# Forgetting attention in pairs of heads: rows 0 to 63 and 64 to 127 of the array, and norm-spreading products over all 128 rows

## The chip, the cores and the metric

The kernel runs on one core of a Trainium2 chip, in one launch. The metric is the device time of that launch in microseconds, and the median of three runs is compared. TensorE (PE in the profile) multiplies, VectorE is DVE, ScalarE is ACT, GpSimd is POOL, and SyncE (SP) issues the loads of the weights. PSUM, where products land, has eight banks.

## The reference

Ten sublayers work on 256 tokens of 1024 channels: feed-forward, forgetting attention ("fox"), two feed-forwards, dilated attention ("dil"), a feed-forward, and then twice a mixing layer and a second kind of feed-forward. The change is about the attention. For each of 16 heads of 64 channels, forgetting attention computes

```python
q, k = rms_norm(q) * q_gain, rms_norm(k) * k_gain      # each head by itself, 64 channels
F = cumsum(log_sigmoid(x @ w_f + b_f))                 # one running sum per head
logits = q @ k.T / 8 + F[queries, None] - F[None, keys]
out = softmax(where(key <= query, logits, -inf)) @ v
```

Dilated attention has the same norm of each head's queries and keys, with three sets of them, and no running sums.

## The kernel before

Activations stand with channels on the 128 partitions and tokens along the free axis. A weight tile is split into a part that float32r holds (`whi`) and the rest (`wlo`), and so are the activations (`hh`, `hl`), so that each float32 product is three float32r ones of 128x256. Each such triple stands in the trace as `banks<-hh,whi`, `hl,whi` and `hh,wlo` (or `whi,hh`, and `oh`, `ol` for attention's outputs). 1024 KB of weights come at a time from SP's queue, four loads ahead; ACT makes `whi` and DVE `wlo`, up to seven units ahead of PE. These projections are the main stream of PE.

What is not a projection runs beside them, as generators. After every few projections `step` asks each generator whether it can emit its next instructions; it asks a planner (`Clock`), which keeps an estimate of each engine's time from shapes alone. So the program order on each engine follows from that estimate, and a change of one generator moves others too. Every instruction is issued by one helper, so that all lines of the trace are L415 (L416 in the changed kernel, where comments went).

In `fox`, a pair of heads shares one tile of queries and keys: head 2c on partitions 0 to 63, head 2c + 1 on 64 to 127. `head_in` squares it and transposes the squares (`cst,hsq`) for the mean squares. `head_norm` works out 1 / rms for two pairs at once (three in `dil`), transposes it (`cst,ypad`), and spreads it over the channels by products with 0/1 matrices: for each pair two products `banks<-yz,sel` of 128x256, of which eight rows of the array are used (rows 32i to 32i + 7 for pair i). There are 8 such pairs in `fox` and 24 in `dil`, 64 products in all.

`fox_head` then does one head: for two tiles of queries, q times k over 64 rows (`banks<-qk`, 64x128 and 64x256; a float32 product is two instructions on PE) and a bfloat16 product over 6 rows that adds the running sums (`banks<-ar` 6x128 and 6x256, tiles E and F, which `fox_sums` fills by small DMAs on POOL's queue); DVE adds the mask and takes the row's maximum; ACT takes the exponential with its sum; three transposes (`cst,ar` 128x128), which ACT copies to `pT`; values times `pT` into 64 partitions of PSUM (`pv`: `ar` 128*64, four instructions); and the inverse sums brought to the same shape (`inverse`: `cst,rs`, four instructions). `turn` lets one head at a time through the part from the transposes on, since there is one `pT`. `o_store` scales the outputs of a pair (`ot`), splits them into `oh` and `ol`, and `attn_out` multiplies them with four chunks of weights; chunk c waits for the pairs 2c and 2c + 1.

Of the kernel before, what the change touches and what calls it, by code (L numbers as in the profile page):

```python
# [66 lines left out]
def _weights(seg):  # L67
    """Chunks of one part of the network, each of one or two units: (key, number of units)."""
# [58 lines left out]

# which layer's modulation is worked out beside which of the first blocks
# [102 lines left out]
# columns of the tile that holds one value per channel  # L231
# [9 lines left out]
# columns of the tile of constants  # L241
_CST = {}
_n = 0
for _name, _w in (("ident", 128), ("ones", 1), ("two", 2), ("part", 1), ("perm", 128), ("causal", 384), ("nc", 256), ("ns", 256), ("cmask", 32), ("valid", 2), ("invf", 1),
# [5 lines left out]
# columns of the small matrices of a mixing layer  # L250
# [8 lines left out]
def _ch(v):  # L259
    """[..., n * 128] -> [128, prod(...) * n]"""  # L260
# [30 lines left out]
def _host_cst():  # L291
# [16 lines left out]
    row = np.arange(128) % 32  # L308
    sel = [(row[:, None] < 8) & (row[:, None] % 4 == w * 2 + np.arange(128)[None, :] // 64) for w in range(2)]
# [5 lines left out]
    c["nc"] = np.cos(ang)[:, d % 32].T  # L315
    c["ns"] = np.sin(ang)[:, d % 32].T * np.where(d < 32, -1.0, 1.0)[:, None]
# [15 lines left out]
    return np.ascontiguousarray(np.concatenate([c[n].reshape(128, w) for n, (_, w) in _CST.items()], axis=1), np.float32), dm, sel  # L332
# [62 lines left out]
class Engine:  # L395
    """An engine's instructions, with an estimate of when they are done."""
# [24 lines left out]
class Clock:  # L421
    """Passes instructions on to the core's engines, and estimates (in ns) when their operands are there and
# [1846 lines left out]
```

## Time and profile before

| | us |
|---|---|
| median of 3 runs (1941.72 to 1943.92) | 1943.55 |
| profiled execution, span | 1946.9 |
| PE busy (97%) | 1891.6 |
| DVE busy (76%) | 1488.4 |
| ACT busy (52%) | 1013.4 |
| forgetting attention, from the norm's scale to the last sum | about 222 to 379 |
| dilated attention, the same | about 771 to 1115 |

The profile is of one execution, whose span is 3.35 us above the median of the runs. A matmul's duration in it is modelled and includes the time through the array, so that busy time says little of how fast matmuls follow each other. The distance from one start to the next does.

### The profile page before, as it was taken

How to read it: one execution, taken by the hardware profiler on the slowest of the kernel's cores; microseconds unless marked ns; L12 is line 12 of the kernel's file. 1: busy time of each engine (PE TensorE's matmuls, PEld its weight loads, DVE VectorE, ACT ScalarE, POOL GpSimd, SP SyncE). 2: the span in 40 equal slices, each digit the busy share in tenths (PEclk: the TensorE clock that was granted, in tenths of full speed). 3: DMA queues.
4: the chain of work that ended last, by engine and by line, in shares of the span. 5: the costliest groups of instructions: out<-in, count | busy, mean ns of one | idle time of the engine just before them, and what ended most of it. 6: DMA issues, size and time to landing. Idle time of an engine off the chain costs nothing.

```text
span 1946.9 us, 36564 instructions
## 1 busy us (share of the span) xinstructions
PE 1891.6 (97%) x15150; PEld 1814.4 (93%) x15150; DVE 1488.4 (76%) x2706; ACT 1013.4 (52%) x1721; POOL 35.5 (2%) x40
## 2 busy tenths in 40 slices
PE   6999999999999999999999999999999998999997
PEld 6999987899999999999989899999889998989997
DVE  6987795598779876767777585569779778969876
ACT  3534644554355445554455464444666555466553
POOL 0100000000000000000000000000000000000000
PEclk9999989999999999999999999999989998999998
DMA  9798373289858973433324175535236543325550
GB/s 373 298 350 322 131 282 109 93 306 362 326 178 298 341 298 130 174 115 125 130 88 143 74 261 205 212 130 188 94 128 217 186 157 127 137 84 191 199 195 23
DMA packets 54167, 378.67 MB, mean 194 GB/s; under 512 B 6096, under 2 KB 7600, under 8 KB 9072
## 3 DMA queue, kind: packets, MB, share of 16 engines
q1 hardware_dynamic: 52992, 373.20, 52.2%
q0 software_dynamic: 864, 3.00, 0.5%
q8 instruction: 118, 1.93, 0.4%
q14 instruction: 49, 0.40, 0.1%
q10 hardware_dynamic: 144, 0.13, 0.0%
HBM read 375.21 MB, written 1.05 MB: 193 GB/s over the span
## 4 chain that ended last, share of the span: by engine, by line
PE 72%; issue 20%; DVE 4%; ACT 2%; POOL 1%; DMA 0%; POOLq 0%; SPq 0%; DVEq 0%; ACTq 0%
PE banks L415 72%; DVE ar L415 1%; DVE wlo L415 1%; POOL rz L415 1%; DVE x L415 1%; ACT whi L415 1%; ACT hh L415 0%; DVE sq L415 0%; DMA x<-x 0%; DVE hl L415 0%; DVE ht L415 0%; ACT sq L415 0%; ACT L415 0%; DVE wraw L415 0%; ACT ar L415 0%
## 5 line engine op out<-in xcount | busy, mean ns | idle before, releaser
L415 PE MATMUL banks<-hh,whi 128*128 128x256 f32 (+1 forms) x2792 | 799.2, 286 | 7.6 <-ACT hh L415 4.7
L415 DVE TENSOR_TENSOR wlo<-wraw,whi 128x1024 fp32r<-128x1024 f32 x557 | 670.2, 1220 | 171.2 <-ACT whi L415 170.6
L415 PE MATMUL banks<-hh,wlo 128*128 128x256 f32 (+1 forms) x2792 | 789.4, 283 | 2.0 <-DVE wlo L415 2.0
L415 PE MATMUL banks<-hl,whi 128*128 128x256 f32 (+1 forms) x2792 | 790.1, 283 | 0.2
L415 ACT CAST whi<-wraw 128x1024 fp32r<-128x1024 f32 x557 | 570.3, 1048 | 177.5 <-DMA wraw<-w 92.2
L415 PEld LDWEIGHTS banks<-hh,whi 128*128 128x128 f32 x2792 | 531.2, 190 | 13.5 <-ACT hh L415 5.5
L415 PEld LDWEIGHTS banks<-hh,wlo 128*128 128x128 f32 x2792 | 531.2, 190 | 2.8 <-DVE wlo L415 2.8
L415 PEld LDWEIGHTS banks<-hl,whi 128*128 128x128 f32 x2792 | 531.4, 190 | 1.1 <-DVE hl L415 1.1
L415 PE MATMUL banks<-oh,whi 128*128 128x256 f32 x1312 | 372.7, 284 | 7.3 <-DVE x L415 3.8
L415 PE MATMUL banks<-ol,whi 128*128 128x256 f32 x1312 | 366.8, 280 | 0.0
L415 PE MATMUL banks<-oh,wlo 128*128 128x256 f32 x1312 | 366.4, 279 | 0.0
L415 PEld LDWEIGHTS banks<-oh,whi 128*128 128x128 f32 x1312 | 247.2, 188 | 14.0 <-DVE x L415 6.3
L415 PEld LDWEIGHTS banks<-ol,whi 128*128 128x128 f32 x1312 | 247.5, 189 | 0.2 <-DVE ol L415 0.2
L415 PEld LDWEIGHTS banks<-oh,wlo 128*128 128x128 f32 x1312 | 247.2, 188 | 0.0
L415 DVE CUSTOM_DVE_ANT_0 wraw<-wraw,cb 128x1024 f32<-128x1024 f32 x128 | 152.0, 1217 | 0.5 <-DMA wraw<-w 0.5
L415 ACT ACTIVATE sg<-banks 128x256 f32<-128x256 f32 x82 | 31.5, 385 | 175.4 <-PE banks L415 175.3
L415 PE MATMUL banks<-whi,hh 128*128 128x256 f32 x352 | 106.0, 301 | 1.6 <-ACT hh L415 1.4
L415 PE MATMUL banks<-whi,hl 128*128 128x256 f32 x352 | 101.3, 288 | 0.1
L415 PE MATMUL banks<-wlo,hh 128*128 128x256 f32 x352 | 100.9, 287 | 0.0
L415 ACT COPY ar<-banks 128x384 f32<-128x384 f32 (+5 forms) x110 | 47.4, 477 | 99.3 <-PE banks L415 96.0
L415 PE MATMUL banks<-ar 128*64 128x256 f32 (+4 forms) x456 | 90.9, 335 | 0.0
L415 DVE SCALAR_TENSOR_TENSOR cy<-cs,vec,cy 128x255 f32<-128x255 f32 (+1 forms) x176 | 83.7, 481 | 7.8 <-ACT cy L415 4.7
(204 smaller groups left out, 1790.5 us busy)
## 6 DMA issues: line engine op xcount, KB each, us to landing
wraw<-w SPq DMA_DIRECT2D x342, 1024.0 KB, 4.9
ar<-w SPq DMA_DIRECT2D x8, 1024.0 KB, 10.4
wraw<-w SPq DMA_DIRECT2D x5, 512.0 KB, 3.4
ar<-lw POOLq DMA_DIRECT2D x2, 752.0 KB, 5.0
x<-x SPq DMA_DIRECT2D x1, 1024.0 KB, 7.2
out<-x SPq DMA_DIRECT2D x8, 128.0 KB, 1.9
cst<-cst SPq DMA_DIRECT2D x1, 595.5 KB, 6.1
ar<-dm POOLq DMA_DIRECT2D x1, 576.0 KB, 10.4
```

The source lines that it names most:

```text
L415: return f(out, *args, **kw)
```

## The change

- `fox_heads` takes the place of `fox_head` and does two heads: the products of head 2c (rows 0 to 63) and of head 2c + 1 (rows 64 to 127) alternate, into two neighbouring banks of PSUM. E and F have the running sums of a pair on partitions 0 to 5 and 64 to 69, zeros elsewhere in each half, so these products take 64 rows.
- `pv2` and `inverse2` alternate between the two heads too, which fill partitions 0 to 63 and 64 to 127 of one bank.
- The transposes come before the wait for `turn`, and there are two `pT`s, each for a pair.
- The products that spread the norms take all 128 rows: `sel` holds, for each pair, zeros but for that pair's rows (768 columns, not 256), and the unused rows of `ypad` are transposed along.
- The DMAs of E and F are 12 of 4 KB, not 6 of 8 KB, and the fills of E and F six, not two. The tables of the rotation leave the constants (256 KB less there) and are loaded into `cb` when the first mixing layer begins; `sel` is loaded and copied with 256 KB more. Comments went.

```diff
-    sel = [(row[:, None] < 8) & (row[:, None] % 4 == w * 2 + ...) for w in range(2)]
+    sel = [(row // 32 == i) & (row % 32 < 8) & (row % 4 == w * 2 + ...)
+           for i in range(3) for w in range(2)]
...
     def head_norm(self, qks, v):
-        m = 32 * n
         for tt in range(2):
-            nc.tensor.transpose(yT[:m, tt * 128:tt * 128 + 128],
-                                yp[:, tt * n:tt * n + n].rearrange("p x c -> p (x c)"), self.c("ident"))
+            nc.tensor.transpose(yT[:, tt * 128:tt * 128 + 128],
+                                self.ypad[:, tt * n:tt * n + 4].rearrange("p x c -> p (x c)"), self.c("ident"))
...
-                nc.tensor.matmul(rb[:, w * S:w * S + S], self.sel[32 * i:32 * i + 8, w * 128:w * 128 + 128],
-                                 z[32 * i:32 * i + 8], start=True, stop=True)
+                nc.tensor.matmul(rb[:, w * S:w * S + S], self.sel[:, (2 * i + w) * 128:(2 * i + w) * 128 + 128],
+                                 z, start=True, stop=True)
...
+    def inverse2(self, out, rs):
+        for qt in range(2):
+            for e in range(2):
+                self.nc.tensor.matmul(out[64 * e:64 * e + 64, qt * 128:qt * 128 + 128],
+                                      rs[:, 2 * e + qt:2 * e + qt + 1].to_broadcast([128, 64]), self.c("ident"), ...)
...
-    def fox_head(self, h, qk, fv, vready, E, F, pvs):
+    def fox_heads(self, c, qk, fv, vready, E, F, pvs):
-        L = yield from self.bank()
+        L = yield from self.bank(2)
         for qt, c0, n in blocks:
             q = slice(qt * 128, qt * 128 + 128)
-            nc.tensor.matmul(L[:, c0:c0 + n], qk[r, q], qk[r, S:S + n], start=True, stop=False)
-            nc.tensor.matmul(L[:, c0:c0 + n], E[:, h, q], F[:, h, :n], start=False, stop=True)
+            for e, r in enumerate(half):
+                nc.tensor.matmul(L[:, e, c0:c0 + n], qk[r, q], qk[r, S:S + n], start=True, stop=False)
+            for e, r in enumerate(half):
+                nc.tensor.matmul(L[:, e, c0:c0 + n], E[r, c, q], F[r, c, :n], start=False, stop=True)
...
-        while self.turn != h:
+        for e in range(2):
+            yield from self.on("pe", P[:, e])
+            ... three transposes, ACT's copy into pT[:, e]
+        while self.turn != c or not vready[c // 2]:
             yield
...
+    def pv2(self, out, parts):
+        for i, (v, pT, kt) in enumerate(parts):
+            for e in range(2):
+                o = out[64 * e:64 * e + 64]
+                q, p = (o[:, 128:S], pT[:, e, 256:384]) if kt else (o[:, :S], pT[:, e, :256])
+                self.nc.tensor.matmul(q, v[e], p, start=i == 0, stop=i == len(parts) - 1, ...)
...
-            nc.gpsimd.dma_start(E[3 + i:4 + i], part[:, :S])
-            nc.gpsimd.dma_start(F[i:i + 1], part[:, S:])
+            for e in range(2):
+                o = 64 * e + i
+                nc.gpsimd.dma_start(E[o + 3:o + 4], part[e:16:2, :S])
+                nc.gpsimd.dma_start(F[o:o + 1], part[e:16:2, S:])
...
+        if l == 0:
+            nc.gpsimd.dma_start(self.cb[:, :2 * S], self.a["turn"])
...
-                k.nc.gpsimd.dma_start(k.ar[:, 0:256], k.a["sel"])
-                k.nc.scalar.copy(k.sel, k.ar[:, 0:256])
+                k.nc.gpsimd.dma_start(k.ar[:, 0:768], k.a["sel"])
+                k.nc.scalar.copy(k.sel, k.ar[:, 0:768])
```

PE, where a head's output products (`ar`), its inverse sums (`rs`), the next head's transposes (`cst,ar`) and logits (`qk`, and `ar` for E and F) follow each other, before:

```order
L415 MATMUL banks<-ar 64x256
L415 MATMUL banks<-ar 64x128
L415 MATMUL banks<-cst,rs 64x128 x2
L415 MATMUL banks<-cst,ar 128x128 x3
L415 MATMUL banks<-qk 128x128
L415 LDWEIGHTS ar
L415 MATMUL banks<-ar 128x128
L415 MATMUL banks<-qk 128x256
L415 LDWEIGHTS ar
L415 MATMUL banks<-ar 128x256
```

PE at the same work now, the output products of one pair (the last of them) and the logits of a later pair:

```order
L416 MATMUL banks<-ar 64x128 x2
L416 MATMUL banks<-cst,rs 64x128 x4
L416 MATMUL banks<-qk 128x128 x2
L416 LDWEIGHTS ar
L416 MATMUL banks<-ar 128x128
L416 LDWEIGHTS ar
L416 MATMUL banks<-ar 128x128
L416 MATMUL banks<-qk 128x256 x2
L416 LDWEIGHTS ar
L416 MATMUL banks<-ar 128x256
L416 LDWEIGHTS ar
L416 MATMUL banks<-ar 128x256
```

The two heads of a pair alternate row by row, and the transposes have moved away from between outputs and logits. Twice in the middle of the stage the outputs of two pairs and the logits of the next two pairs stand in one run like this.

ACT, the exponentials (`ar,sums<-ar,nm`) of the fifth and the sixth pair and the copies of their transposes, now:

```order
L416 ACTIVATE ar,sums<-ar,nm 128x128
L416 ACTIVATE ar,sums<-ar,nm 128x256
L416 ACTIVATE ar,sums<-ar,nm 128x128
L416 ACTIVATE ar,sums<-ar,nm 128x256
L416 COPY ar<-banks 128x384
L416 ACTIVATE ar,sums<-ar,nm 128x128
L416 ACTIVATE ar,sums<-ar,nm 128x256
L416 ACTIVATE ar,sums<-ar,nm 128x128
L416 ACTIVATE ar,sums<-ar,nm 128x256
L416 COPY ar<-banks 128x384
```

Before, the exponentials of one head (two rows) stood between copies; now those of four heads stand nearly in a row, and PE has six projections between two of the heads' transposes.

DVE at the end of dilated attention, from the last head's inverse sums (`rs`) to the split of the last outputs (`ot`, `ol`), before:

```order
L415 RECIPROCAL rs<-sums 128x2
L415 TENSOR_TENSOR wlo<-wraw,whi 128x1024 x2
L415 TENSOR_TENSOR ot<-ot 128x256
L415 TENSOR_TENSOR ol<-ot,oh 128x256
L415 SCALAR_TENSOR_TENSOR x<-banks,modc,x 128x256 x2
```

And now:

```order
L416 RECIPROCAL rs<-sums 128x2
L416 TENSOR_TENSOR wlo<-wraw,whi 128x1024
L416 TENSOR_TENSOR modc<-modr,vec 128x8 x2
L416 SCALAR_TENSOR_TENSOR modc<-modc,vec 128x8
L416 TENSOR_TENSOR hl<-modc,hh 128x8x2
L416 TENSOR_TENSOR wlo<-wraw,whi 128x1024
L416 TENSOR_TENSOR ot<-ot 128x256
L416 TENSOR_TENSOR wlo<-wraw,whi 128x1024
L416 TENSOR_TENSOR ol<-ot,oh 128x256
```

One `wlo` has come between `ot` and `ol`. On PE, the products of the last chunk (48) followed the last inverse sums directly before; now 36 products of the chunk ahead of it stand between the two.

## Rows read from the trace of the kernel before

**Rows 1.** Stretches: busy us per engine, granted clock (PEclk), DMA share, GB/s.

```profile
274.80:285.04 10.24, 10.24 (x45) 9.33 (x44) 9.96 (x31) 3.92 (x10) 0.00 (x0) 0.50 0.63 236
285.00:375.00 90.00, 90.00 (x595) 70.54 (x594) 46.34 (x137) 44.91 (x114) 0.00 (x0) 1.00 0.34 120
```

**Rows 2.** PE in order of time, 315.5 to 319: start, us, operation, count.

```profile
315.51 0.28 PE L415 MATMUL banks<-wlo,hh 128*128 128x256 f32 x1
315.63 0.28 PE L415 MATMUL banks<-whi,hl 128*128 128x256 f32 x1
315.84 0.86 PE L415 MATMUL banks<-ar 128*64 128x256 f32 x4
316.54 0.60 PE L415 MATMUL banks<-cst,rs 128*64 128x128 f32 x4
317.07 0.55 PE L415 MATMUL banks<-cst,ar 128*128 128x128 f32 x3
317.55 0.48 PE L415 MATMUL banks<-qk 64*128 64x128 f32 x2
317.96 0.22 PE L415 MATMUL banks<-ar 6*128 6x128 bf16 x1
318.12 0.70 PE L415 MATMUL banks<-qk 64*128 64x256 f32 x2
318.75 0.28 PE L415 MATMUL banks<-ar 6*128 6x256 bf16 x1
318.96 0.66 PE L415 MATMUL banks<-cst,hsq 128*128 128x128 f32 x4
```

**Rows 3.** PE around the logits of the first two heads, same view.

```profile
271.09 0.28 PE L415 MATMUL banks<-hh,wlo 128*128 128x256 f32 x1
...
274.12 0.39 PE L415 MATMUL banks<-whi,hh 128*128 128x256 f32 x1
```

**Rows 4.** Dilated attention's logits: one head in order of time.

```profile
1005.17 2.23 PE L415 MATMUL banks<-qk 64*128 64x128 f32 x12
1007.33 0.38 PE L415 MATMUL banks<-hh,whi 128*128 128x256 f32 x1
```

**Rows 5.** Stretches of `qk` on PE alone, busy and count: one head, then two.

```profile
1050.25:1051.00 0.75, 0.75 (x5) 1.00 0.00 0
1051.64:1052.39 0.75, 0.75 (x9) 1.00 0.27 44
```

**Rows 6.** A mixing layer's products into halves of the partitions, in order of time.

```profile
1332.90 1.14 PE L415 MATMUL banks<-ar,sv 128*64 128x128 f32 x16
```

**Rows 7.** PE around one pair's products with `sel`, in order of time.

```profile
1036.61 0.28 PE L415 MATMUL banks<-hh,wlo 128*128 128x256 f32 x1
1036.82 0.50 PE L415 MATMUL banks<-yz,sel 8*128 8x256 f32 x2
...
1037.46 0.28 PE L415 MATMUL banks<-hl,whi 128*128 128x256 f32 x1
```

**Rows 8.** PE in order of time at the end of dilated attention.

```profile
1104.36 0.28 PE L415 MATMUL banks<-oh,wlo 128*128 128x256 f32 x1
1107.79 0.58 PE L415 MATMUL banks<-oh,whi 128*128 128x256 f32 x1 [3.15 <-ACT oh L415]
```

**Rows 9.** The stretch of half clock there, columns as in rows 1.

```profile
1107.65:1111.06 3.41, 3.27 (x14) 3.10 (x15) 1.60 (x4) 0.77 (x3) 0.00 (x0) 0.50 0.82 300
```

**Rows 10.** Groups, 250 to 380: count, busy us, mean ns, idle before.

```profile
L415 ACT ACTIVATE ar<-ar,nm 128x256 f32<-128x256 f32 x16 | 7.9, 497 | 0.0
L415 ACT ACTIVATE ar<-ar,nm 128x128 f32<-128x128 f32 x16 | 6.4, 403 | 0.0
```

**Rows 11.** POOL in order of time: the last two DMAs of E and F.

```profile
260.56 0.96 POOL L415 DMA_DIRECT2D ar<-fpart  x2 [7.93 <-ACT fpart L415]
```

**Rows 12.** DMA issues of E and F: count, KB each, median us to landing.

```profile
ar<-fpart POOLq DMA_DIRECT2D x6, 8.0 KB, 4.9
```

**Rows 13.** ACT's copy of the norm's spread scale, in order of time: idle before it.

```profile
222.55 0.37 ACT L415 COPY rb<-banks 128x256 f32<-128x256 f32 x1 [3.44 <-PE banks L415]
```

More of the change, by code (lines that the diff above doesn't have):

```diff
@@ L243 @@
 _n = 0
-for _name, _w in (("ident", 128), ("ones", 1), ("two", 2), ("part", 1), ("perm", 128), ("causal", 384), ("nc", 256), ("ns", 256), ("cmask", 32), ("valid", 2), ("invf", 1),
+for _name, _w in (("ident", 128), ("ones", 1), ("two", 2), ("part", 1), ("perm", 128), ("causal", 384), ("cmask", 32), ("valid", 2), ("invf", 1),
                   ("sgn", 1), ("triu", 128)):
@@ L307, in _host_cst @@
     dm = np.ascontiguousarray(np.concatenate(d0 + d1, axis=1), np.float32)
-    row = np.arange(128) % 32
-    sel = [(row[:, None] < 8) & (row[:, None] % 4 == w * 2 + np.arange(128)[None, :] // 64) for w in range(2)]
+    row = np.arange(128)[:, None]
+    sel = [(row // 32 == i) & (row % 32 < 8) & (row % 4 == w * 2 + np.arange(128)[None, :] // 64)
+           for i in range(3) for w in range(2)]
     sel = np.ascontiguousarray(np.concatenate(sel, axis=1), np.float32)
@@ L331, in _host_cst @@
     c["ones"] = np.ones((128, 1))
-    return np.ascontiguousarray(np.concatenate([c[n].reshape(128, w) for n, (_, w) in _CST.items()], axis=1), np.float32), dm, sel
+    return np.ascontiguousarray(np.concatenate([c[n].reshape(128, w) for n, (_, w) in _CST.items()], axis=1), np.float32), dm, sel, turn
 def _host_lw(a):
@@ L681, in __init__ @@
         self.ar = c.tile([128, AR], F32, name="ar")
-        self.sel = c.tile([128, 256], F32R, name="sel")
+        self.sel = c.tile([128, 768], F32R, name="sel")
         self.rb = c.tile([128, S], F32, name="rb")
-        self.ypad = c.tile([128, 6, 32], F32, name="ypad")
+        self.ypad = c.tile([128, 7, 32], F32, name="ypad")
         self.half = c.tile([128, 8], F32, name="half")
@@ L1280, in head_norm @@
             for w in range(2):
-                nc.tensor.matmul(rb[:, w * S:w * S + S], self.sel[32 * i:32 * i + 8, w * 128:w * 128 + 128],
-                                 z[32 * i:32 * i + 8], start=True, stop=True)
+                nc.tensor.matmul(rb[:, w * S:w * S + S],
+                                 self.sel[:, (2 * i + w) * 128:(2 * i + w) * 128 + 128], z,
+                                 start=True, stop=True)
             yield from self.on("dve", rb)
@@ L1330, in fox_norm @@
             ready[i] = "out"
-    def fox_head(self, h, qk, fv, vready, E, F, pvs):
+    def fox_heads(self, c, qk, fv, vready, E, F, pvs):
         nc = self.nc
         cm = self.c("causal")
-        e = h % 2
-        r = slice(64 * e, 64 * e + 64)
-        P, pT = self.PP[e], self.PT
-        while e in self.busy:
+        half = [slice(0, 64), slice(64, 128)]
+        P, pT = self.PP[c % 2], self.PT[c % 2]
+        while c % 2 in self.busy:
             yield
-        self.busy.add(e)
-        nm, sm, rs = self.small(2, "nm"), self.small(2, "sums"), self.small(2, "rs")
+        self.busy.add(c % 2)
+        nm, sm, rs = self.small(4, "nm"), self.small(4, "sums"), self.small(4, "rs")
@@ new lines, in fox_heads @@
+            for e, r in enumerate(half):
+                nc.tensor.matmul(L[:, e, c0:c0 + n], E[r, c, q], F[r, c, :n], start=False, stop=True)
+        for e in range(2):
+            yield from self.on("dve", L[:, e, 0:384], out=[P[:, e]])
+            for qt, c0, n in blocks:
+                nc.vector.tensor_tensor_reduce(P[:, e, c0:c0 + n], L[:, e, c0:c0 + n], cm[:, c0:c0 + n], -1.0, CAP,
+                                               OP.add, OP.min, nm[:, 2 * e + qt:2 * e + qt + 1])
+        self.rel(L)
@@ L1359, in fox_head @@
+        self.logits += 2
+        for e in range(2):
+            yield from self.on("act", P[:, e])
+            for qt, c0, n in blocks:
+                i = slice(2 * e + qt, 2 * e + qt + 1)
+                nc.scalar.activation(P[:, e, c0:c0 + n], P[:, e, c0:c0 + n], AF.Exp, scale=-1.0, bias=nm[:, i],
+                                     accum_out=sm[:, i])
         yield from self.on("dve", sm)
         nc.vector.reciprocal(rs, sm)
-        while self.turn != h:
-            yield
-        yield from self.on("pe", P)
@@ L1364, in fox_head @@
-        T = yield from self.bank()
-        for i in range(3):
-            nc.tensor.transpose(T[:, i * 128:i * 128 + 128], P[:, i * 128:i * 128 + 128], self.c("ident"))
-        self.busy.remove(e)
-        yield from self.on("act", T[:, :384], out=[pT])
-        nc.scalar.copy(pT, T[:, :384])
-        self.rel(T)
-        yield from self.on("pe", pT, rs)
-        while not vready[h // 4]:
-            yield
-        pv = yield from self.pv_bank(h, pvs)
-        self.pv(pv[r, :S], [(fv[:, kt, h * 64:h * 64 + 64], pT[:, :384], kt) for kt in range(2)])
@@ L1376, in fox_head @@
-        self.turn = h + 1
-        self.inverse(pv[r, S:], rs)
-        if e:
-            yield from self.o_store(pvs, h, h // 2, True)
-            self.stored.add(h // 2)
+        for e in range(2):
+            yield from self.on("pe", P[:, e])
+            T = yield from self.bank()
+            for i in range(3):
+                nc.tensor.transpose(T[:, i * 128:i * 128 + 128], P[:, e, i * 128:i * 128 + 128], self.c("ident"))
+            yield from self.on("act", T[:, :384], out=[pT[:, e]])
+            nc.scalar.copy(pT[:, e], T[:, :384])
+            self.rel(T)
@@ new lines, in fox_heads @@
+        while self.turn != c or not vready[c // 2]:
+            yield
+        yield from self.on("pe", pT, rs)
+        pv = yield from self.bank()
+        self.pv2(pv, [([fv[:, kt, (2 * c + e) * 64:(2 * c + e) * 64 + 64] for e in range(2)], pT, kt) for kt in range(2)])
+        self.inverse2(pv[:, S:], rs)
+        self.busy.remove(c % 2)
+        self.turn = c + 1
+        pvs[c] = pv
+        yield from self.o_store(pvs, 2 * c, c, True)
+        self.stored.add(c)
+    def pv2(self, out, parts):
+        for i, (v, pT, kt) in enumerate(parts):
+            for e in range(2):
+                o = out[64 * e:64 * e + 64]
+                q, p = (o[:, 128:S], pT[:, e, 256:384]) if kt else (o[:, :S], pT[:, e, :256])
+                self.nc.tensor.matmul(q, v[e], p, start=i == 0, stop=i == len(parts) - 1, skip_group_check=True)
@@ L1391, in fox @@
         fv = self.ar[:, 0:2048].rearrange("p (t n) -> p t n", t=2)
-        E, F = (self.ar[:6, o:o + 2048].bitcast(BF16).rearrange("p (h t) -> p h t", h=16) for o in (2048, 4096))
-        self.PP = [self.ar[:, 6144 + 384 * i:6528 + 384 * i] for i in range(2)]
-        self.PT = self.ar[:, 6912:7296]
+        E, F = (self.ar[:, o:o + 1024].bitcast(BF16).rearrange("p (c t) -> p c t", c=8) for o in (2048, 3072))
+        two = lambda o: [self.ar[:, o + 768 * i:o + 768 * i + 768].rearrange("p (e n) -> p e n", e=2) for i in range(2)]
+        self.PP, self.PT = two(4096), two(5632)
         pvs = {}
@@ L1397, in fox @@
         self.busy, self.logits, self.turn = set(), 0, 0
-        nc.gpsimd.memset(E, 1.0)
-        nc.gpsimd.memset(F, 1.0)
+        for t in (E, F):
+            nc.gpsimd.memset(t, 0.0)
+            for e in range(2):
+                nc.gpsimd.memset(t[64 * e:64 * e + 6], 1.0)
         self.foxg = self.small(2, "foxg")
@@ L1458, in fox_sums @@
             nc.scalar.copy(part, cum)
-            nc.gpsimd.dma_start(E[3 + i:4 + i], part[:, :S])
-            nc.gpsimd.dma_start(F[i:i + 1], part[:, S:])
+            for e in range(2):
+                o = 64 * e + i
+                nc.gpsimd.dma_start(E[o + 3:o + 4], part[e:16:2, :S])
+                nc.gpsimd.dma_start(F[o:o + 1], part[e:16:2, S:])
             if i < 2:
@@ L2240, in layout @@
     w = np.concatenate([np.ascontiguousarray(_chunk_data(key, a)).reshape(-1) for key, _ in _plan()])
-    cst, dm, sel = _host_cst()
+    cst, dm, sel, turn = _host_cst()
     return {
@@ L2250, in layout @@
         "sel": sel,
+        "turn": turn,
         "lw": _host_lw(a),
```

34 lines of the change are left out of this document (14 added, 20 removed).

## The prediction

> **What bounds the kernel now.** I read first which engine is full: PE is 97% busy, but a matmul's duration is modelled, so I took the view of stretches and the order of time on PE. From 285 to 375, where forgetting attention's heads are worked on, PE is never idle while DVE and ACT are busy for half the time [rows 1]; the view of waits names none for PE between 250 and 375. What PE does there counts one for one. The projections follow each other every 0.12 us (315.51 to 315.63 in [rows 2]). The heads' products don't. Each time PE goes from products over the whole array to products over a part of it, or between two kinds of part, the next start comes later than the stream of columns needs: 0.21 instead of 0.12 at 315.84 [rows 2]. So a change costs about 0.09, and a head's logits have four of them inside and around the bfloat16 products over 6 rows. In dilated attention PE's one wait until 1108 is at the end: 3.15 us for the last outputs [rows 8]. The granted clock falls to its half level (1.2 GHz) for 10.24 us from 274.80 [rows 1], straight behind the logits of two heads that stand back to back [rows 3], and for 3.41 us from 1107.65 [rows 9], behind the wait just named.
>
> **Logits.** One head, 317.55 to 318.96, takes 1.41, with the change ahead of it 1.5 [rows 2]; the first two take 274.12 - 271.09 - 0.12 = 2.91, or 1.45 each [rows 3]. 16 x 1.45 = 23.2 us. In the changed kernel all of a pair's logits are over 64 rows, so the changes inside go. What streams for one head: in dilated attention three sets of 64x128 and 64x256 take 1007.33 - 1005.17 = 2.16, less 0.2 at both ends, 0.65 a set [rows 4]; the bfloat16 products are 0.16 and 0.21 from start to next start, less 0.1 each for the change, 0.17 together [rows 2]. That is 0.82. Whether the two heads run at the same time is shown by dilated attention, where the second of two adjacent heads starts on the other 64 rows before the first is done: nine products start in a stretch in which five start for one head alone [rows 5]. So a pair takes 0.82, 0.2 for the ends and 0.1 for the second half's later start: 1.12, 9.0 in all. **Gain 14.2.** If the halves took turns, it would be 1.84 a pair, and the gain 8.5.
>
> **Outputs and inverse sums.** One head takes 317.07 - 315.84 = 1.23 and 0.09 for the change ahead: 16 x 1.32 = 21.1. The four inverse products take 0.53 with the change behind, so 0.11 for 128 columns and twice that for 256 [rows 2]: 2 x 0.21 + 6 x 0.11 = 1.08 of streaming. The two heads fill different halves of the partitions of one bank. A mixing layer has such products, alternating between the halves: 16 of them in 1.14 us, where 16 x 0.11 would be 1.76 [rows 6]; there too the halves run together for most of the time. So 1.08 + 0.2 + 0.1 = 1.38 a pair, 11.0 in all. **Gain 10.1**; 2.2 if the halves took turns.
> A rule of the Trainium skill speaks against this gain: TensorE: Matmul & The Clock Gate, under Part 3, The mechanism, says that loading weights overlaps with a running matmul only where the rows differ, and here both halves take all 128 rows. By that rule the sum would take the 2.2; the sixteen products of [rows 6] don't agree with it.
>
> **Products that spread the norms.** From the projection ahead to the second one behind, a pair of them takes 1037.46 - 1036.61 = 0.85, where four steps of 0.12 are 0.48 [rows 7]. Over all rows they are like any projection, and 0.37 goes, 32 times: **gain 11.8**, 24 parts of 32 in dilated attention. Where the neighbour is itself on part of the array, a part of the 0.37 is paid anyway; with 0.3 it is 9.6. The transposes of `ypad` with 128 rows stream the same columns: nothing, at either end of 0.1 us each.
>
> **The end of dilated attention.** As [rows 8] show, 3.43 us pass between two products that would be 0.12 apart. The new order puts 36 products between the last inverse sums and the chunk that waits, 36 x 0.12 = 4.3 us, and one more `wlo` ahead of the last `ol`. The cover is 0.9 longer than the wait, the `wlo` some 1.2 longer: I leave 0.5 of the wait, **gain 2.7**. PE's idle time ahead of the fall at 1107.65 goes, so I take the fall as gone: half of 3.41 [rows 9], **gain 1.7**, or nothing.
>
> **The clock in forgetting attention.** 10.24 us at the half level lose 5.1 us [rows 1]. What stood ahead were 2.9 us of half-empty products; now 2.2 us with both halves busy. Later heads fill runs with half an array (315.84 to 318.96, [rows 2]) and the clock stays up [rows 1]. I take the fall as gone: **gain 5.1**, between nothing and that.
>
> **New waits.** The planner now puts exponentials of four heads on ACT in a row; one head's take 0.40 + 0.50 [rows 10]. From a pair's last logits PE has, in the narrowest place, 1.12 of the next pair and six projections, 1.9 us, until it wants the transposes of the first head, which need the mask on DVE and 0.9 on ACT behind the copies of outputs: a wait of some 0.7; the second head's follow 0.9 later each. Three such places: **loss 3**, between 0 and 8.
>
> **At nothing.** Six more DMAs for E and F put the last issue 1 us later, 262.5 for 261.5, landing 4.9 later, at 267.4 [rows 11, 12]; the first logits start after 271 [rows 3]. If that cover went, PE would wait for what is missing. POOL's fills stand there long before attention, and the next norm's power behind them is not due. The copy of `sel`, some 0.5 longer on ACT, lies ahead of 3.44 us in which ACT waits for PE [rows 13]. The tables of the rotation, 256 KB, are loaded a layer's start ahead of their use; only the fill behind them on POOL waits, for one issue.
>
> **Sum.** 14.2 + 10.1 + 11.8 + 2.7 + 1.7 + 5.1 - 3 = 42.6 us against the profiled execution's span of 1946.9: 1904.3. The runs lie 3.35 below it, so 1901. After the gain DVE and ACT, half idle there [rows 1], are not the next limit.
>
> **Rivals.** (a) The column halves take turns: weights of one half wait for the other's products. 7.9 less gain, 1909; and the row halves too, 5.7 less again, 1914. [rows 5, 6] speak against both.
> (b) The halves run together, and the clock falls anyway, at the first logits or at one of the long runs of outputs and logits: 5.1 each, 1906 with one fall, 1911 with two. For it: the one fall there is stood behind logits [rows 1, 3]. Against it: the new runs keep both halves busy.
> (c) The heads' chain becomes the bound: exponentials and copies on ACT hold up the transposes after each pair. Eight pairs at 0.9 + 0.5 are 11 us rather than 3: 1909. Against it: ACT is idle for half the stretch [rows 1].
> (d) Slower: products over parts of the array hold the clock at its half level through the whole of the heads' stretch. Each fall costs 5.1, the gain without the clock's share there is 37.5, so from eight falls on, 82 us, there is nothing left; with nine it is 1947. Against it: with more changes and half the array empty it fell once [rows 1].
> (e) The change doesn't do what it says only if (a) holds for both halves; `sel` and the order at the end of dilated attention would still give 1914.
>
> **How the numbers follow.** The forecast, 1901 with its own bounds (waits 0 to 8, `sel` 9.6): 0.58. (a) 0.10, (b) 0.17, (c) 0.10, (d) 0.02, and 0.03 for a time near the one before or above it by what the planner moved elsewhere. A difference of 0.2%, 3.9 us, is about what a measurement here can tell from none. Faster by more than that: 0.96; within it 0.02; slower 0.02. The range takes the forecast's lower bound with no new wait and two microseconds of other falls of the clock that shift, 1895, up to 1914, where (a) and (c) end.
>
> **What would show it.** In the trace after: two heads' `qk` starting within 0.02 us of each other and a pair's logits in 1.1 to 1.2 us; outputs and inverse sums of a pair in 1.3 to 1.4; 0.12 between the starts around `yz,sel`; no half clock near 275 or near 1107; PE's waits before `cst,ar` summing to less than 8 us. It is wrong if the pairs take 1.8 and 2.4, if the clock falls in the runs of outputs and logits, or if projections wait for `wlo` where DVE's masks now come in bursts.

## The result

The changed kernel takes 1899.4 us (median of 4 runs, 1898.17 to 1902.38) where the kernel before takes 1943.74 in the same comparison (1941.72 to 1946.37): a ratio of 0.977, 95% interval 0.975 to 0.978. 44.3 us are gone. The profiled executions differ by 46.3, 1946.9 to 1900.6 of span. In every run on record the launch's time is about 1.8 us above its span (1902.38 and 1900.6 for the changed kernel's profiled one). So the execution of before that was profiled took about 1948.7 us, an estimate from that difference, 5 above the median of its runs; the 3.35 us between its span and that median compare two different measures.

The page of the changed kernel: busy time by engine, and the granted clock in 40 slices.

```profile
PE 1848.5 (97%) x15150; PEld 1794.1 (94%) x15150; DVE 1485.6 (78%) x2698; ACT 1013.8 (53%) x1721; POOL 42.9 (2%) x51
...
PEclk9999999999999999999999999999999998999999
```

PE is still full; what went is work that lay on it. To place the 46 us I cut the traces where POOL computes `rz`, the scale of each block's norm. The starts that enclose forgetting attention and dilated attention, before and then in the changed kernel (start, us, operation, and in brackets how long POOL was idle before):

```profile
220.11 1.64 POOL L415 TENSOR_TENSOR rz<-var,half 128x2 f32<-128x2 f32 x1 [160.08 <-DVE var L415]
...
385.02 1.57 POOL L415 TENSOR_TENSOR rz<-var,half 128x2 f32<-128x2 f32 x1 [123.49 <-DVE var L415]
...
765.83 1.64 POOL L415 TENSOR_TENSOR rz<-var,half 128x2 f32<-128x2 f32 x1 [187.75 <-DVE var L415]
1121.10 1.54 POOL L415 TENSOR_TENSOR rz<-var,half 128x2 f32<-128x2 f32 x1 [353.63 <-DVE var L415]
```

```profile
219.51 1.57 POOL L416 TENSOR_TENSOR rz<-var,half 128x2 f32<-128x2 f32 x1 [157.19 <-DVE var L416]
...
351.82 1.57 POOL L416 TENSOR_TENSOR rz<-var,half 128x2 f32<-128x2 f32 x1 [90.71 <-DVE var L416]
...
732.56 1.63 POOL L416 TENSOR_TENSOR rz<-var,half 128x2 f32<-128x2 f32 x1 [187.71 <-DVE var L416]
1074.70 1.55 POOL L416 TENSOR_TENSOR rz<-var,half 128x2 f32<-128x2 f32 x1 [340.50 <-DVE var L416]
```

Forgetting attention: 351.82 - 219.51 = 132.3 us, before 385.02 - 220.11 = 164.9, so 32.6 less. Dilated attention: 1074.70 - 732.56 = 342.1, before 1121.10 - 765.83 = 355.3, so 13.1 less. Everything else differs by under 1 us together. The same two lengths for every kernel of this study, beside the runs' median:

| kernel | us | forgetting | dilated | half clock in forgetting |
|---|---|---|---|---|
| before | 1943.7 | 164.9 | 355.3 | 10.24 |
| before, another execution | 1945.0 | 163.4 | 355.3 | 6.83 |
| changed | 1899.4 | 132.3 | 342.1 | none |
| heads apart, wide `sel` | 1930.8 | 158.0 | 346.8 | none |
| the same, another execution | 1933.8 | 159.6 | 346.1 | 3.41 |
| heads apart, sums over 64 rows | 1920.1 | 152.8 | 342.2 | none |
| pairs, `sel` over 8 rows | 1912.3 | 135.4 | 351.2 | none |
| pairs, logits in turn | 1901.9 | 133.7 | 342.2 | none |
| pairs, outputs in turn | 1905.1 | 136.9 | 342.2 | none |
| pairs, both in turn | 1905.0 | 138.6 | 342.2 | none |
| pairs, sums over 6 rows | 1902.6 | 135.5 | 342.2 | none |
| dilated outputs in pairs too | 1887.1 | 132.2 | 326.1 | none |
| and dilated logits | 1881.0 | 132.3 | 322.0 | none |
| with 8 masks, not 12 | 1879.1 | 132.2 | 319.1 | none |

The changed kernel's answers to the rows of before, PE in order of time: a pair's logits (for [rows 2, 3]), a pair's outputs and inverse sums (for [rows 2]), one of the two places where two pairs' outputs and two pairs' logits stand in one run, and two products with `sel` (for [rows 7]).

```profile
318.05 0.28 PE L416 MATMUL banks<-oh,wlo 128*128 128x256 f32 x1
318.25 0.49 PE L416 MATMUL banks<-qk 64*128 64x128 f32 x4
318.58 0.22 PE L416 MATMUL banks<-ar 64*128 64x128 bf16 x2
318.63 0.66 PE L416 MATMUL banks<-qk 64*128 64x256 f32 x4
319.12 0.28 PE L416 MATMUL banks<-ar 64*128 64x256 bf16 x2
319.33 0.39 PE L416 MATMUL banks<-oh,whi 128*128 128x256 f32 x1
319.55 0.28 PE L416 MATMUL banks<-ol,whi 128*128 128x256 f32 x1
...
307.91 0.87 PE L416 MATMUL banks<-ar 128*64 128x256 f32 x8
308.61 0.61 PE L416 MATMUL banks<-cst,rs 128*64 128x128 f32 x8
309.15 0.66 PE L416 MATMUL banks<-cst,hsq 128*128 128x128 f32 x4
...
286.88 0.87 PE L416 MATMUL banks<-ar 128*64 128x256 f32 x8
...
289.20 0.49 PE L416 MATMUL banks<-qk 64*128 64x128 f32 x4
...
291.15 0.39 PE L416 MATMUL banks<-hh,whi 128*128 128x256 f32 x1
...
274.03 0.28 PE L416 MATMUL banks<-whi,hl 128*128 128x256 f32 x1
274.15 0.40 PE L416 MATMUL banks<-yz,sel 128*128 128x256 f32 x2
274.39 0.28 PE L416 MATMUL banks<-whi,hh 128*128 128x256 f32 x1
```

Twice the instructions (x4 for x2, x8 for x4) stand in less time: the logits of two heads take 319.33 - 318.25 = 1.08 us, where one took 1.41; outputs and inverse sums of two take 1.24, where one took 1.23. Of two adjacent pairs, the outputs take 289.20 - 286.88 = 2.32 and the logits 291.15 - 289.20 = 1.95. The starts of the two heads' products lie 0.007 us apart. The products with `sel` now follow like projections, 0.12 apart.

### The profile page after: what moved, and what is told of

Read it like the earlier page. It is cut to its first block, busy times and chain, and to the rows that moved or that the text cites. A ratio compares the mean times of both kernels' runs of the same rounds, so it can differ in the third digit from the quotient of the medians.

```text
span 1900.6 us, 36573 instructions
## 1 busy us (share of the span) xinstructions
PE 1848.5 (97%) x15150; PEld 1794.1 (94%) x15150; DVE 1485.6 (78%) x2698; ACT 1013.8 (53%) x1721; POOL 42.9 (2%) x51
## 4 chain that ended last, share of the span: by engine, by line
PE 81%; issue 11%; DVE 4%; ACT 2%; POOL 1%; DMA 0%; POOLq 0%; SPq 0%; DVEq 0%; ACTq 0%
PE banks L416 81%; POOL rz L416 1%; DVE x L416 1%; DVE wlo L416 1%; ACT whi L416 1%; DVE ar L416 1%; DVE sq L416 1%; ACT hh L416 0%; ACT ar L416 0%; DVE hl L416 0%; ACT sq L416 0%; DMA x<-x 0%; DVE ht L416 0%; ACT L416 0%; DVE rs L416 0%
## 5 line engine op out<-in xcount | busy, mean ns | idle before, releaser
L416 DVE TENSOR_TENSOR sg<-banks,sg 128x256 f32<-128x256 f32 x82 | 34.4, 422 | 66.6 <-ACT sg L416 66.5
```

The costliest lines, as they stand in the source:

```text
L416: return f(out, *args, **kw)
```

## The experiments

**Heads one at a time again, `sel` wide.** The old `fox_head` in the changed kernel, so that only the products that spread the norms, and what is loaded for them and for the rotation, differ from before.

```diff
-                    self.pending.append((lambda ready=ready, i=i: ready[i] == "out",
-                                         self.fox_heads(c - 1 + i, qks[i], fv, vready, E, F, pvs)))
+                    self.pending.append((lambda ready=ready, j=i // 2: ready[j] == "out",
+                                         self.fox_head(2 * c - 2 + i, qks[i // 2], fv, vready, E, F, pvs)))
```

> The changed kernel with forgetting attention's heads one at a time again, as before the change; only the products that spread the norms keep all 128 rows. Theory (the sum of the prediction): of the gain 11.8 us stay (0.37 for each of 32 pairs of products; 9.6 by the lower bound), the wait at the end of dilated attention and both falls of the clock are back, so 1932 us, 1930 to 1935, and the granted clock is 0.50 from about 275 and from about 1104. Rival 1, the falls and the wait at the end of dilated attention had to do with the narrow products that spread the norms: then they stay away here, 10 us more are gained, about 1922. Rival 2, a product over 8 rows costs no more than one over 128: no gain, 1943.

1930.8 us (ratio 0.992 to 0.995): 12.3 less than before, where 11.8 were expected. The wait at the end of dilated attention is there, as in [rows 8], and with it the half clock, 3.41 us from 1088.45 (PE's waits by releaser, 720 to 1110: us in total, times, longest):

```profile
PE banks L416 <- ACT oh L416: 3.2, 1, 3.2
```

So the pairs, with the sums over 64 rows and what both move, are worth the other 31 us. But the clock did not fall in forgetting attention in this execution, which the theory had wanted, so a part of the 12.3 may be the clock's; the next run gives the price of the 8 rows without it, and two more executions below return to the fall.

**`sel` over 8 rows, pairs kept.**

```diff
-                                 self.sel[:, (2 * i + w) * 128:(2 * i + w) * 128 + 128], z,
+                                 self.sel[32 * i:32 * i + 8, (2 * i + w) * 128:(2 * i + w) * 128 + 128], z[32 * i:32 * i + 8],
```

> The changed kernel with the products that spread the norms over 8 rows again (8 partitions of sel and yz for each pair); everything else, and PE's order, as changed. Theory: 32 pairs of products cost 0.37 us more each, 11.8 in all (9.6 by the lower bound), 24 of them in dilated attention: 1909 to 1911 us, with no wait for the last outputs and no fall of the clock at the end of dilated attention, since the order there stays. Rival (what dilated attention gained, 13 us, came from the order at its end, and rows hardly count): 1900 to 1903.

1912.3 us (ratio 0.981 to 0.985). Forgetting attention gets 3.1 us longer and dilated attention 9.1: 0.38 for each of the 8 and 24 parts. The rival falls; the number of rows is the price, and the order at the end of dilated attention, which is that of the changed kernel here, has nothing to do with it.

**Logits in turn, outputs in turn, both.** The planner still counts the products in alternating order, so that everything else stands where it stood; they are only issued head by head.

```diff
+        self.held = None
+
+    def in_turn(self):
+        calls, self.held = self.held, None
+        for f, a, kw in calls[0::2] + calls[1::2]:
+            f(*a, **kw)
...
+            if self.held is not None:
+                self.held.append((f, (out,) + args, kw))
+                return
             return f(out, *args, **kw)
...
+        nc.tensor.held = []
         self.pv2(pv, [([fv[:, kt, (2 * c + e) * 64:(2 * c + e) * 64 + 64] for e in range(2)], pT, kt) for kt in range(2)])
         self.inverse2(pv[:, S:], rs)
+        nc.tensor.in_turn()
```

> The changed kernel, with the same products in the same place of PE's order, but of each pair's logits all of head 0's first, then all of head 1's. In the changed kernel a pair's logits take 0.98 us from the first start to the next projection but one. Theory (the halves run at the same time, and that is the larger part of the gain): in turn a pair takes 1.6 to 1.8, 8 pairs lose 5 to 6.5 us, 1905 us; up to 1910 if the clock falls again near 275 as it did behind logits that filled half the array. Rival (the gain came from keeping one kind of part of the array, without the changes in between, and the halves take turns in any order): a pair stays at about 1.0 and the time at 1899 to 1900.

> The changed kernel, with the same products in the same place of PE's order, but of each pair's outputs and inverse sums all of head 0's first, then all of head 1's. In the changed kernel they take 1.14 to 1.18 us a pair. Theory (column halves run at the same time): in turn 2.0 to 2.2, 8 pairs lose 7 to 8 us, 1907 us. Rival (the weights of one half wait for the other half's products anyway, and what was gained is one change of the array's part less for each head): 1.2 to 1.4 stay, 1899 to 1901.

> The changed kernel, with the same products in the same place of PE's order, but in each pair both logits and outputs of head 0 ahead of those of head 1. Theory: the two losses add, 5 to 6.5 and 7 to 8, so 1912 to 1914 us, and if half-empty products bring the fall of the clock near 275 back (10 us at the half level), 5 more, 1917 to 1919. Rival (only the number of changes of the array's part counted): 1899 to 1901.

1901.9, 1905.1 and 1905.0 us (ratios 0.977 to 0.980, 0.979 to 0.981, 0.979 to 0.982). All lose less than expected, the logits least: 1.4 us in the stage for 5 to 6.5 (both together 6.3 for 12 to 14.5). The reason is in the traces. (The 0.98 and 1.14 to 1.18 of the expectations are the distance from one pair to the next where two are adjacent; a pair by itself takes 1.08 and 1.24.) First logits in turn, then outputs in turn, PE in order of time:

```profile
318.26 0.48 PE L406 MATMUL banks<-qk 64*128 64x128 f32 x2
318.59 0.22 PE L406 MATMUL banks<-ar 64*128 64x128 bf16 x1
318.59 0.70 PE L406 MATMUL banks<-qk 64*128 64x128 f32 x4
...
319.66 0.38 PE L425 MATMUL banks<-oh,whi 128*128 128x256 f32 x1
```

```profile
310.35 0.86 PE L406 MATMUL banks<-ar 128*64 128x256 f32 x4
311.05 0.27 PE L406 MATMUL banks<-cst,rs 128*64 128x128 f32 x1
311.05 0.43 PE L406 MATMUL banks<-ar 128*64 128x256 f32 x1
311.16 0.38 PE L406 MATMUL banks<-cst,rs 128*64 128x128 f32 x2
...
312.29 0.55 PE L425 MATMUL banks<-cst,hsq 128*128 128x128 f32 x3
```

A head's outputs and inverse sums are eight entries of the trace (each float32 product is two), four `ar` and then four `rs`. Head 1's first entry, `ar` over 256 columns, is the ninth in the order of issue, and it starts at 311.05, ahead of the sixth (`rs` at 311.16). PE does not wait for head 0's last three. With the logits the same: head 1's `qk` over 128 columns, the seventh, starts at 318.59 (the second row with that time, in which entries of both heads are merged), 0.05 ahead of head 0's first `qk` over 256, the fourth. So issuing head by head does not make the halves take turns; it sets the second head back, by 0.33 us in the logits and by 0.70 in the outputs (where head 0's four `ar` and its first `rs` go ahead). A pair goes from 1.08 to 319.66 - 318.26 = 1.40 and from 1.24 to 312.29 - 310.35 = 1.94. The outputs come near the 2.0 to 2.2 expected, with 4.6 us lost in the stage, and show that the column halves run side by side in the changed kernel; the logits' run tests little of what it was made for.

**Sums over 6 rows in pairs.**

```diff
-                nc.tensor.matmul(L[:, e, c0:c0 + n], E[r, c, q], F[r, c, :n], start=False, stop=True)
+                nc.tensor.matmul(L[:, e, c0:c0 + n], E[64 * e:64 * e + 6, c, q], F[64 * e:64 * e + 6, c, :n], start=False, stop=True)
```

> The changed kernel, but the products of the forget gates' sums take 6 rows of each half (partitions 0 to 5 and 64 to 69) and not 64, so that within a pair's logits the kind of part changes again three times inside and once behind, two heads still side by side. Theory: each change costs about 0.09 us as before the change, 8 pairs with four of them lose 3 us, 1902 us. Rival (the changes were the larger part of the gain in the logits, because they also keep the halves from running at the same time): a pair goes from 0.98 to 1.8 or more, 1906 to 1908. Second rival (6 rows of a half count as that half): 1899.

1902.6 us (ratio 0.976 to 0.980), as the theory had it. One pair, PE in order of time:

```profile
321.52 0.49 PE L416 MATMUL banks<-qk 64*128 64x128 f32 x4
321.94 0.23 PE L416 MATMUL banks<-ar 6*128 6x128 bf16 x2
322.10 0.70 PE L416 MATMUL banks<-qk 64*128 64x256 f32 x4
322.74 0.28 PE L416 MATMUL banks<-ar 6*128 6x256 bf16 x2
322.95 0.39 PE L416 MATMUL banks<-oh,whi 128*128 128x256 f32 x1
```

The two heads still start together (x4, x2); from `qk` to the products over 6 rows it is 0.42 instead of 0.33, and a pair takes 322.95 - 321.52 = 1.43 instead of 1.08. The three changes more cost 0.35: 0.09 the first, as in [rows 2], and 0.12 each on average. They delay both heads at once, and don't keep the halves apart.

**Sums over 64 rows, heads apart.** The other half of that test, on the kernel with heads apart.

```diff
-            nc.tensor.matmul(L[:, c0:c0 + n], E[:, h, q], F[:, h, :n], start=False, stop=True)
+            nc.tensor.matmul(L[:, c0:c0 + n], E[r, h // 2, q], F[r, h // 2, :n], start=False, stop=True)
```

> The kernel of the run with heads one at a time and wide products for the norms (1931 us; its logits take 1.41 us a head from the first start to the next product over the whole array), with the forget gates' sums over the 64 rows of the head's half instead of 6: no change of the part of the array inside a head's logits, still no pair. Theory (the gain in the logits has two parts, the changes inside a head and the two halves side by side): a head takes 1.05 to 1.1, 16 heads gain 5 to 6 us, 1925 to 1926 us, and about 8 us of the logits' gain belongs to the halves running together. Rival 1 (the changes were all of it): 0.7 to 0.8 a head, 11 us, 1920. Rival 2 (products over 64 rows that carry 6 useful ones cost as much as the changes): no gain, 1931.

1920.1 us (ratio 0.986 to 0.989), 10.7 less than with 6 rows; rival 1 has that number, but not its reason. One head, PE in order of time:

```profile
288.95 0.49 PE L416 MATMUL banks<-qk 64*128 64x128 f32 x2
...
290.02 0.50 PE L416 MATMUL banks<-yz,sel 128*128 128x256 f32 x2
```

A head alone takes 290.02 - 288.95 = 1.07, as the theory had it, and forgetting attention is 5.3 us shorter. Another 4.6 went in dilated attention, where nothing was edited: with heads apart over 6 rows, as in the kernel before, the chunk that waits for the last outputs stands three products behind the last inverse sums (not directly behind), and in this kernel the planner came out with 36 more ahead of it, as in the changed kernel, and the wait is absent. And one head alone takes as long as a pair in the changed kernel (1.07 and 1.08). That splits the gain in the logits: 16 x (1.41 - 1.07) = 5.4 us belong to the changes inside a head, 8 x 1.07 = 8.6 to two heads in the time of one. The split depends on the order: taken first with 6 rows, the pairs are worth 8 x (2.82 - 1.43) = 11.1, and the 64 rows then 8 x 0.35 = 2.8.

**The clock, two more executions.**

> The kernel before, unchanged, for a second look at the granted clock in forgetting attention. The run with heads one at a time has the same logits in the same place, two heads over half the array back to back, and shows no fall near 270. Theory of the prediction (the back-to-back logits of two half-empty heads take the clock down): the 10 us at 0.50 near 275 are there again. Rival (the fall depends on when that stretch of PE comes, not on what stands in it, so it comes and goes between executions): it is missing or at another place, and the span is about 5 us shorter.

> The kernel with heads one at a time and wide products for the norms, a second time, for the granted clock in forgetting attention. In two executions of the kernel before the clock fell there, at 274.80 and 274.61, behind the first two heads' logits from 271.30 and 271.05; in the first execution of this kernel, with the same logits from 268.65, it did not. If what stands there decides (the same half-empty logits, but no narrow products for the norms behind them), there is again no fall. If only the moment decides, and the logits start nearer to 271 this time, the fall is there, and the span is 3 to 5 us longer than 1927.

The kernel before falls again, from 274.61 for 6.83 us; the one with heads apart, which had not fallen, does now, from 273.67 for 3.41, behind logits that began at 270.45. Windows from about the fall on, of before and of heads apart, then the same place in the changed kernel (us of the stretch, busy PE, PEld, DVE, ACT, POOL, granted clock, DMA share, GB/s):

```profile
274.00:282.00 8.00, 8.00 (x37) 7.09 (x38) 7.72 (x26) 4.55 (x11) 0.00 (x0) 0.57 0.81 318
```

```profile
273.00:277.00 4.00, 4.00 (x21) 3.83 (x21) 4.00 (x10) 3.98 (x6) 0.00 (x0) 0.58 1.00 395
```

```profile
272.00:277.00 5.00, 5.00 (x49) 4.51 (x48) 5.00 (x7) 2.57 (x4) 0.00 (x0) 1.00 0.99 405
```

Three of four profiled executions with two half-empty heads back to back (6 rows in their sums) fell to the half level (1.2 GHz) right behind them, for 10.24, 6.83 and 3.41 us; no profiled execution of the other ten kernels did, though the changed kernel's first logits stand at 271.39. So the fall goes with these logits, not always, and the moment alone does not bring it. The moment may have a part: the second execution with heads apart came out as its rival had it, with logits nearer to 271, the fall, and a span 4.6 longer (1932.0 for 1927.4), and the one execution without a fall had its logits earliest. Whether the empty half does it, or the changes to 6 rows, is not separated. What a fall costs can be read from the table: 3.41 us more of it make the stage 1.5 us longer in either kernel (164.9 for 163.4, 159.6 for 158.0). That it lasts longer where narrow products with `sel` follow (10.24 and 6.83) than where wide ones do (3.41 and none) is two executions each, and stays open.

**A step further: dilated attention in pairs.** Three kernels, which give the outputs, then the logits too, the same treatment.

```diff
+        self.pv2(pv, [([dv[:, g, kt, vh[e]] for e in range(2)], pT[:, :, g * 384:g * 384 + 384], kt)
+                      for g in range(3) for kt in range(2)])
+        self.inverse2(pv[:, S:], rs)
...
+            for c0, n in ((0, 128), (128, 256)):
+                for e, r in enumerate(half):
+                    nc.tensor.matmul(L[:, e, c0:c0 + n], qk[r, c0:c0 + 128], qk[r, S:S + n], start=True, stop=True)
```

> A step beyond the changed kernel: dilated attention too takes the outputs and inverse sums of two heads at a time, in the two column halves; logits stay one head at a time. The mask is kept once, in bfloat16, to make room for a second head's transposes. In the changed kernel one head's outputs and inverse sums take 828.00 to about 830.53 and 0.1 for the change ahead, 2.63 us. Theory: a pair takes about as long as a head did, 8 times 2.6 go, 21 us, 1878 us. Rival (the chain of a pair, masks on DVE, exponentials and six copies on ACT, now ends in bursts, and PE waits for it): each pair gives back 1 to 2 us, 1886 to 1895; if the pairs are also no longer worked on ahead, nothing is left, 1899 or more.

> As the run before, and the logits of two heads of dilated attention side by side in the row halves as well, one dilation after another in two banks each (which takes 8 more reductions on DVE for each pair and one that joins their minima). In the changed kernel one head's logits take 2.15 us (816.88 to 819.03) and 0.1 for the change ahead. Theory: a pair takes about as long as a head did, with up to 0.4 more where projections come between the dilations, so 8 times 1.9 to 2.2 go, 15 to 18 us beyond the run before: 1860 to 1863 us. Rival (DVE, three quarters busy in dilated attention, and the chain behind it bound): no gain over the run before, 1878 to 1890, with PE waiting for DVE there.

> As the run that took logits and outputs of dilated attention in pairs (1881 us, where PE waited 5.8 us for the norms behind DVE's masks), but a pair's logits are laid out over two banks so that DVE makes 8 reductions for a pair and not 12, and one minimum of two. Theory (DVE's 12 masks in a row held up the norms, which held up PE): the waits for the norms fall to 2 us or less, 1876 to 1878 us. Rival (the waits come from the order in which the pairs are worked on, not from DVE's work): 1880 to 1882.

1887.1, 1881.0 and 1879.1 us (ratios 0.968 to 0.972, 0.965 to 0.969, 0.965 to 0.968): all beat the changed kernel, all by less than the theory. A pair's outputs in the first, a pair's logits in the second, then PE's waits at the end of dilated attention in the first, in all of it in the second and the third, and for the third the longest wait and the stretch of half clock (columns as in [rows 1]):

```profile
838.26 2.17 PE L416 MATMUL banks<-ar 128*64 128x256 f32 x24
...
840.80 0.44 PE L416 MATMUL banks<-cst,hsq 128*128 128x128 f32 x2
```

```profile
811.91 2.24 PE L416 MATMUL banks<-qk 64*128 64x128 f32 x24
```

```profile
PE banks L416 <- ACT ar L416: 2.6, 2, 1.5
PE banks L416 <- ACT oh L416: 1.0, 1, 1.0
```

```profile
PE banks L416 <- DVE ypad L416: 5.8, 3, 2.0
```

```profile
PE banks L416 <- DVE qk L416: 5.2, 1, 5.2
PE banks L416 <- DVE ypad L416: 1.6, 2, 1.0
```

```profile
1008.62 0.58 PE L416 MATMUL banks<-oh,whi 128*128 128x256 f32 x1 [5.21 <-DVE qk L416]
```

```profile
1006.59:1013.42 6.83, 4.80 (x22) 4.81 (x23) 6.61 (x14) 2.15 (x4) 0.00 (x0) 0.50 0.31 128
```

The pairs are as cheap as forecast: 840.80 - 838.26 = 2.54 for two heads' outputs, what one takes in the changed kernel, and 2.24 of busy time for two heads' logits (2.23 for one in [rows 4]). The first kernel's stage is 16.0 us shorter, not 21: 3.6 are waits for ACT, since the last pair now comes as a lump with nothing behind it. The second's is 4.1 shorter than that, not 15 to 18: the masks come in lumps on DVE and the norms behind them come late (5.8); the rest of the miss is only in part placed. Four reductions less for each pair bring these waits to 1.6, below the 2 of the theory, but then one wait of 5.2 appears near the end, and the clock falls in it, for 6.83 us. The product that waits, the first of attention's outputs with the weights (`oh,whi`, 1008.62), doesn't read the `qk` it waits for. By the program `attn_out` takes four banks at once, and DVE's operation on this `qk`, which ends 0.06 us ahead, frees one; that the wait is for the bank is read from this and not tested. So the third kernel and the second are the same within their intervals, though the third's stage is 2.9 shorter.

## Why the prediction held

Forecast 1901 with 1895 to 1914, measured 1899.4. The mechanism is the one forecast, but the number came nearer than the sum. The sum had 42.6 us, and the spans differ by 46.3: dilated attention gave 13.1 where the steps for it add up to 13.3, forgetting attention 32.6 for 29.4. Then 3.35 was taken off to get from a span to the median of the runs, where the changed kernel's span is 1.2 above the median. 3.7 too little gain and 2.1 too much taken off leave 1.6, and that they cancel is luck. By the steps:

- **Logits**, gain 14.2 forecast. The heads ran side by side. The 8 pairs take three times 1.95 for two adjacent ones and twice 1.08, with 0.09 ahead of three of these groups 8.3 us, for 9.0 forecast. The 23.2 of the working for before is too small: it takes for every head the 1.45 of the first two, while the other fourteen stand alone at 1.41 + 0.09 = 1.50. With these it is 23.9, and the gain 15.6. It is right for the reasons given, both shown by the runs above; the working had 8.5 for the changes and 5.7 for the halves side by side, counted from two heads that take turns in one run.
- **Outputs and inverse sums**, 10.1 forecast. Pairs take 1.24, not 1.38, and 2.32 where two are adjacent; with 0.09 ahead 10.1 in all for 11.0: gain 11.0. The rule of the Trainium skill that the prediction set against [rows 6] (TensorE: Matmul & The Clock Gate, Part 3, The mechanism: weights load beside a running product only where the rows differ) does not describe these products: both halves take all 128 rows, and sixteen entries run in 1.24 us where eight took 1.23.
- **Left out of the sum:** the change back to the whole array. Behind a pair the second projection follows after 0.22 (319.33 to 319.55), not 0.12. There were 31 such ends before, and there are 9 now. Behind 17 of the 31 stand products over 128 columns, where it is 0.05 and not 0.10: 2.3 us before, 0.9 now, 1.4 more gain. The working counted the changes ahead of a head and inside, not the one behind.
- **`sel`**, 11.8 forecast: 12.2 by stages. Right, on the rows.
- **End of dilated attention**, 2.7 and 1.7 forecast: 4.6 between the heads-apart kernel and the changed one, 4.1 between before and the changed one with `sel` over 8 rows. Right in size; the wait is gone wholly, and with it the fall. But it belongs to the planner's order, which another edit upstream moved just as well.
- **Clock in forgetting attention**, 5.1 forecast: the fall is gone. The 5.1 took half of 10.24 for lost; at 1.5 us for 3.41, as the two more executions give it, it is 4.6, an estimate. What it is worth depends on the execution, 0 to 4.6.
- **New waits**, 3 forecast. PE's waits from 215 to 380 that the kernel before doesn't have, two short ones for the pairs' transposes and one of attention's outputs, by releaser and then the row of the longest:

```profile
PE banks L416 <- DVE yz L416: 1.2, 1, 1.2
...
PE banks L416 <- ACT ar L416: 0.5, 2, 0.3
```

```profile
315.48 0.39 PE L416 MATMUL banks<-oh,whi 128*128 128x256 f32 x1 [1.19 <-DVE yz L416]
```

1.7 us. In the place that the prediction had priced, the transposes behind the exponentials, there are 0.5, so the term of 3 was too large and its place is hardly one. The other was not foreseen: the first product of the outputs with the weights waits for DVE's `yz` of a norm, which it doesn't read. As in the last of the runs above, that fits the four banks that `attn_out` takes at once, one of which the norm frees then; no run tests it.

Added up for forgetting attention, 15.6 + 11.0 + 1.4 + 3.1 + 4.6 - 1.7 = 34.0, where the stage lost 32.6: 1.4 us are not placed. Of the rivals, (a) fell by the starts 0.007 apart, (b) and (d) by the clock, which fell there in no profiled execution with pairs, (c) by 0.5 us of waits for ACT.

## What to carry to other kernels

Products that fill half the array should come in pairs on the other half, and products over few rows or columns should be padded to the shape of their neighbours: here two heads cost what one did, and each change of shape avoided was worth about 0.1 us on a full PE. Price such a change by runs of products from the last product of the whole array to the second one behind, or the change back is missed. Issue the two halves alternately: head by head cost 0.33 us a pair in the logits and 0.70 in the outputs. Pairs make the work of the other engines come in lumps; what it costs shows where a stage ends and nothing is left to put in between.

## What the hardware showed beyond that

- PE starts products on the free half of the array ahead of earlier ones on the other half: the ninth entry of a pair's outputs at 311.05, ahead of the sixth at 311.16; the seventh of the logits 0.006 us behind the third and 0.05 ahead of the fourth. In both cases three entries of the first head were passed. This is the start that the trace records; the ends are modelled.
- Where both heads' sums took rows from the same half (partitions 0 to 5, before the change), the second head did not start early: two adjacent heads took 2.82 us, twice 1.41. With the sums over each head's own 64 rows two adjacent heads, issued one after the other, took 1.40. That run moved the rows and did away with the changes to 6 rows at once, so which of the two lets the second head go ahead is not shown.
- A half-empty stretch of 2.8 us was followed by a fall of the clock for 10.24, 6.83, 3.41 us or not at all, in four executions with the same logits there.
